# A norm's inverse roots spread through memory, another norm's chain pinned, and the first weights laid side by side, in a hybrid attention layer

## Chip, cores and metric

One core of one Trainium2 chip runs the whole layer. The time is device microseconds of the execution; the median of several runs counts. A profiled execution, taken by the hardware profiler, gives the trace. TensorE is called PE here, VectorE DVE, ScalarE ACT, GpSimd POOL and SyncE SP.

## What is computed

One encoder layer on a sequence of 1024 tokens, width 1024, in float32:

```python
hn = rmsnorm(h, norm_mix)
proj = hn @ w_in                         # 1024 -> 2304, columns for two groups of heads
o_a = window_gqa_sink(rope(qa), rope(ka), va, sink)   # 8 heads, |i-j| <= 128, 2 key heads
o_b = neighbourhood_attention(qb, kb, vb, rpb)        # 8 heads on a 16 x 64 grid
mix = concat([rmsnorm(o_a, norm_a), rmsnorm(o_b, norm_b)])
h = h + mix @ w_out
hn = rmsnorm(h, norm_ffn)
h = h + conv_gated_mlp(hn, w_gate, w_up, conv_w, conv_b, w_down)
return rmsnorm(h, norm_final)

def rmsnorm(x, g):
    return x * rsqrt(mean(x * x, axis=-1) + 1e-6) * g
```

## The kernel before

Everything is held transposed: features lie on the 128 partitions, tokens along the free dimension, so that x is eight tiles of 128x1024 (`KT` = 8). PE multiplies at a reduced float32 precision; the kernel therefore splits each operand into a high part and a low part and makes three products of each pair: high by high, low x by high weights, high x by low weights (`block`, lines 167 to 170). The high part is a copy on ACT, the low part a subtraction on DVE. A tile of 512 tokens (`tsl(h)`, two halves) is the unit of a matmul.

**The order of work.** PE's instructions stand in the order in which the program writes them (`manual_schedule`, line 127). The other engines' instructions are placed by a scheduler, by priority and its own estimate; `tc.high_priority` lifts some, `pin` holds some in program order, and `behind(...)` (line 144) lets an instruction be issued only after a marked one. Each engine executes its own queue strictly in order, SP's queue of DMA issues too, so an instruction that waits holds all behind it.

**The head.** The first three column tiles of `w_in` (`first`, m = 0 to 2) are projected while x arrives. SP issues x and the weights interleaved (lines 88 to 122): the weights of each of the three tiles by themselves, in steps of 1, 1, 2 and 4 row tiles. `split_x` (line 618) makes the two parts of x scaled by the norm's gain, `split_first_w` (line 625) those of the weights, `add_square` (line 631) sums x² over the tiles on ACT and DVE. PE runs nine warming matmuls (`WARM`), then six of the eight row tiles for all three column tiles and both halves (lines 674 to 677). The remaining two (`TAIL`) come tile by tile, and between them stands the first norm: transposes `ss` and a reduce give sums of squares on 128x4 numbers (`inverse_narrow`, line 207), ACT takes the root, DVE the reciprocal, and PE spreads the roots over all partitions by transposes of broadcast columns (`widen`, line 228), `sw` in the trace; ACT copies them to `rstd1`. As the roots are applied after the product (`evacuate`, line 236), the matmuls don't wait for them, but PE's order has `sw` at a fixed place.

**The jobs.** Behind the head stand `jobs`: column tiles 3 to 17 (`Project`) and, as `OutA`, group A's half of the product with `w_out`. `load` fetches and splits the first half of a job's weights, `load_rest` the second; the raw weights have two buffers. The generator `rest` (line 727) hands out the blocks of these jobs one by one, and the attention code pulls them between its own steps, so that PE has work while softmax runs on the other engines. Work of other kinds is hung on fixed blocks of a job by the table `aux` (line 784).

**Between projection and attention.** Tiles of group A are rotated (`rotate`, line 246): DMAs fold the rows on to all partitions (`f<-t`), DVE turns them, DMAs bring them back (`t<-f`). Group B's queries and keys are split and stacked by four DMAs (`split_qk`, line 292). The bias tiles of group B (`bias_tiles`, line 468) are loaded to `rr`, which has one buffer, and built on POOL (`xb`).

**Group A's norm.** After group A's attention, `square_a` sums the squares of four tiles, `narrow_a` adds them up by transposes and takes the inverse roots on 128x8 numbers, `wide_a` spreads them with two sets of PE transposes and two ACT copies to `rstda`, and `normed_a` multiplies each of four tiles, half by half, by gain and root on DVE (lines 757 to 786).

**Tables.** ACT loads a table of functions when it changes from exp to the square root and back.

Of the kernel before, what the change touches and what calls it, by code (L numbers as in the profile page):

```python
# [13 lines left out]
F32 = mybir.dt.float32  # L14
F32R = mybir.dt.float32r
# [21 lines left out]
EVA = (1, 3, 5, 8)  # L37
WARM = 9

# [13 lines left out]

def hybrid_layer(tc, xT, w_in, w_out, w_gate, w_up, w_down, small, sink, rpb, consts, rope, out):
    nc = tc.nc
    with ExitStack() as ctx:
        pool = lambda name, bufs, **kw: ctx.enter_context(tc.tile_pool(name=name, bufs=bufs, **kw))
        cpool = pool("const", 1)
        lpool = pool("long", 1)
        psum = pool("psum", 2, space=PSUM)  # L60
        attention_pools = ctx.enter_context(ExitStack())
        inner = lambda name, bufs: attention_pools.enter_context(tc.tile_pool(name=name, bufs=bufs))
# [28 lines left out]

        def halves(name, dt=F32):
            t = big(name, "mix", dt)[:, :].rearrange("p (k c) -> p k c", c=128)
            return t[:, 0:4], t[:, 4:8]

        raws = [wpool.tile([128, 4, 128], F32, name="raw", tag="raw", bufs=2) for _ in range(2)]
        his, los = ([wpool.tile([128, 4, 128], F32R, name=n, tag=n) for _ in range(3)] for n in ("whi", "wlo"))
        (r3, r3b), r12, h12, l12, (h3, l3) = halves("r3"), halves("r12"), halves("h12", F32R), halves("l12", F32R), halves("w3", F32R)
        head = [list(zip((*raws, r3), his, los)), list(zip((*r12, r3b), (*h12, h3), (*l12, l3)))]

        def load_first_w(m, ks):
            raw, at = head[ks.start // 4][m][0], slice(ks.start % 4, ks.start % 4 + ks.stop - ks.start)
            pin(nc.sync.dma_start(raw[:, at], w_in[m, :, ks, :]))

        steps = [slice(0, 1), slice(1, 2), slice(2, 4), slice(4, 8)]
# [89 lines left out]
        def add_up(v, sq, tag):  # L195

            n = v.shape[-1]
            ps = bank("ss", tag)
            for c in range(n):
                nc.tensor.transpose(ps[:, c * 128:(c + 1) * 128], sq[:, c * 128:(c + 1) * 128], ident)  # L200
            nc.vector.tensor_reduce(v, ps[:, 0:n * 128].rearrange("p (c w) -> p c w", w=128), axis=mybir.AxisListType.X, op=ALU.add)

        def inverse_root(v, dim):
            nc.scalar.activation(v, v, AF.Sqrt, bias=eps, scale=1.0 / dim)
            nc.vector.reciprocal(v, v)

# [84 lines left out]

        def split_qk(t):

            a, b, q = big("ka", "op", F32R), big("kb", "op", F32R), big("q", "op", F32R)
            by = cst[:, K_SCALE:K_SCALE + 1]
            for h in range(2):
                nc.scalar.activation(a[:, tsl(h)], t[:, tsl(h)], AF.Copy, scale=by)
                nc.vector.scalar_tensor_tensor(b[:, tsl(h)], t[:, tsl(h)], by, f32(a[:, tsl(h)]), op0=ALU.mult, op1=ALU.subtract)
            with tc.high_priority(offset=500):
                nc.sync.dma_start(f32(q[0:64, :]), f32(a[0:64, :]))  # L300
                nc.sync.dma_start(f32(q[64:128, :]), f32(b[0:64, :]))
                nc.sync.dma_start(f32(b[0:64, :]), f32(a[64:128, :]))
                nc.sync.dma_start(f32(a[0:64, :]), f32(b[64:128, :]))
            return q, (a, b)
# [64 lines left out]

# [21 lines left out]
        def softmax(st, j, ps, n, bias, nsink=None):  # L391
# [3 lines left out]
            with tc.high_priority(offset=50):  # L395
# [9 lines left out]
                e = n if nsink is None else n + 1  # L405
                nc.scalar.activation(p[:, j, 0:e], p[:, j, 0:e], AF.Exp, bias=nm, scale=-1.0, accum_out=sm[:, j:j + 1])  # L406
                if j == 1:
# [145 lines left out]
        class Project:  # L553
# [3 lines left out]
            def load(self):  # L557
                raw, self.raw = (fetch_w(w_in[self.m, :, k:k + 4, :]) for k in (0, 4))
                self.w = halve_w(raw)
# [64 lines left out]

        def split_first_w(m, ks):
            raw, hi, lo = (t[:, ks.start % 4:ks.start % 4 + ks.stop - ks.start] for t in head[ks.start // 4][m])
            pin(nc.scalar.activation(hi, raw, AF.Copy))  # L627
            pin(nc.vector.tensor_tensor(lo, raw, f32(hi), op=ALU.subtract))
            first[m].w += [(hi[:, j], lo[:, j]) for j in range(ks.stop - ks.start)]

# [12 lines left out]
        for m in range(3):  # L643
            split_first_w(m, steps[0])
        split_x(0, tsl(1))
        for m in range(3):
            split_first_w(m, steps[1])
        for h in range(2):
            split_x(1, tsl(h))
        for m in range(3):  # L650
            split_first_w(m, steps[2])
        acc = add_square(xts[0], None)
        for k in range(2, KT):
            split_x(k)
            if k == 3:
                for m in range(3):
                    split_first_w(m, steps[3])
            acc = add_square(xts[k - 1], acc)
# [193 lines left out]
        for u in range(len(flat)):  # L852
# [14 lines left out]
            for what, e in events:  # L867
# [633 lines left out]
def _layout(inputs):  # L1501
# [9 lines left out]
    rpb[:, ROWS - KH:ROWS + KH - 1] = g["rpb"][0][:, ::-1, ::-1]  # L1511
    consts, rope = _constants()
    arrays = {
        "xT": g["x"][0].T.reshape(KT, 128, S),
        "w_in": blocks(g["w_in"][0][:, _column_order()]),
        "w_out": blocks(g["w_out"][0]),
# [29 lines left out]
```

## Time and profile before

| | us |
|---|---|
| median of 3 runs | 1079.47 (1079.44 to 1079.79) |
| the profiled execution | 1084.39 |
| its span, first to last instruction | 1082.6 |
| PE busy | 1065.0 |
| DVE busy | 867.8 |
| ACT busy | 556.8 |
| POOL busy | 109.9 |
| mean granted clock of TensorE | 0.995 of full speed |

How to read the lines that the prediction shows. In a time line, the first number is the start in us from the start of the span, the second the duration (of all, where several equal ones follow each other: x8), then engine, line of the kernel, operation, what is written <- what is read, shapes, and in brackets the idle time of the engine just before and what ended it. An engine with a q behind it (SPq) is its queue issuing DMAs. Matmuls overlap: the pace is the distance between starts, not the duration. In the list of waits the three numbers are the total in us, how often, and the longest. A row of DMA issues ends with size and median us from issue to landing. A row of windows gives the stretch, its length, the busy time of PE, PEld (weight loads), DVE, ACT and POOL, the granted clock, the busy share of the DMA engines and GB/s.

### The profile page before, as it was taken

The page shows a single profiled execution, that of the slowest core. Times are in us where ns is not written, and L with a number is a line of the kernel's source. Part 1 is how long each engine was busy: PE and PEld are TensorE (multiplying, and loading weights), DVE is VectorE, ACT ScalarE, POOL GpSimd, SP SyncE. Part 2 cuts the span into 40 slices and gives each one's busy share as a digit, 9 for nine tenths or more (in the row PEclk, how much of TensorE's full clock was granted, in tenths as well). Part 3 has the DMA queues.
Part 4 walks back from the last instruction along what each step waited for, and adds up shares of the span by engine and source line. Part 5 has one row for each costly group of instructions (what it writes and reads, how often), then busy time and mean ns, then how long its engine had stood idle before and what let it go on. Part 6 is the DMA issues. An engine that isn't in the chain of part 4 may idle for free.

```text
span 1082.6 us, 14936 instructions
## 1 busy us (share of the span) xinstructions
PE 1065.0 (98%) x5096; PEld 890.0 (82%) x5096; DVE 867.8 (80%) x1599; ACT 556.8 (51%) x1063; POOL 109.9 (10%) x188
## 2 busy tenths in 40 slices
PE   9899999999999999999999999999999999999997
PEld 7688888888888888887788888888888888888886
DVE  6689888667888689899998877877887857897765
ACT  8257777656686545535434334342433645454451
POOL 0323332222233100000000000000000000000001
PEclk9999999999999999999999999999999999999998
DMA  7222122232325146214342222322322789876644
GB/s 276 65 70 70 50 68 69 68 89 68 88 68 163 63 144 244 88 39 165 127 153 101 107 107 97 126 89 108 115 88 98 242 277 309 273 225 231 226 142 156
DMA packets 69084, 144.94 MB, mean 134 GB/s; under 512 B 8208, under 2 KB 19600, under 8 KB 69008
## 3 DMA queue, kind: packets, MB, share of 16 engines
q1 hardware_dynamic: 58784, 118.43, 34.1%
q10 hardware_dynamic: 10224, 25.56, 6.3%
q8 instruction: 40, 0.66, 0.2%
q14 instruction: 36, 0.29, 0.1%
HBM read 103.58 MB, written 28.57 MB: 122 GB/s over the span
## 4 chain that ended last, share of the span: by engine, by line
PE 87%; DVE 8%; DMA 3%; ACT 1%; issue 1%; SPq 0%; POOL 0%; DVEq 0%; ACTq 0%
PE pj L168 7%; PE pj L170 7%; PE pj L169 7%; PE dn L940 6%; PE dn L942 6%; PE dn L941 6%; PE z L942 4%; PE z L940 4%; PE z L941 4%; PE s L380 3%; PE x L940 3%; PE x L941 3%; PE x L942 3%; PE y L942 3%; PE y L940 3%; PE y L941 3%
## 5 line engine op out<-in xcount | busy, mean ns | idle before, releaser
L929 ACT ACTIVATE whi<-ws 128x512 fp32r<-128x512 f32 (+1 forms) x100 | 60.3, 622 | 126.0 <-DVE ws L1047 82.5
L940 PE MATMUL dn<-xd,whi 128*128 128x512 f32 (+1 forms) x330 | 124.0, 376 | 0.0
L942 PE MATMUL dn<-xd,wlo 128*128 128x512 f32 (+1 forms) x330 | 123.7, 375 | 0.0
L941 PE MATMUL dn<-xd,whi 128*128 128x512 f32 (+1 forms) x330 | 123.7, 375 | 0.0
L168 PE MATMUL pj<-xgh,whi 128*128 128x512 f32 x248 | 104.6, 422 | 0.2 <-ACT whi L627 0.2
L942 PE MATMUL z<-hg,wlo 128*128 128x512 f32 x264 | 103.1, 390 | 0.7 <-DVE wlo L930 0.7
L940 PE MATMUL z<-hg,whi 128*128 128x512 f32 x264 | 102.9, 390 | 0.0
L941 PE MATMUL z<-hg,whi 128*128 128x512 f32 x264 | 102.7, 389 | 0.0
L410 POOL TENSOR_SCALAR p<-p,sm 128x384 f32<-128x384 f32 (+1 forms) x128 | 79.8, 637 | 208.6 <-DVE sm L408 167.1
L406 ACT ACTIVATE p<-p,nm 128x385 f32<-128x385 f32 (+3 forms) x128 | 75.2, 587 | 49.8 <-DVE nm L402 48.9
L169 PE MATMUL pj<-xgl,whi 128*128 128x512 f32 x248 | 97.5, 393 | 0.9 <-DVE xgl L623 0.8
L170 PE MATMUL pj<-xgh,wlo 128*128 128x512 f32 x248 | 97.6, 394 | 0.0
L930 DVE TENSOR_TENSOR wlo<-raw,whi 128x512 fp32r<-128x512 f32 (+1 forms) x102 | 66.3, 672 | 26.0 <-ACT whi L929 25.1
L929 ACT ACTIVATE whi<-raw 128x512 fp32r<-128x512 f32 (+1 forms) x102 | 60.5, 612 | 45.5 <-DMA raw<-in_w_down_dram 18.6
L417 DVE TENSOR_TENSOR pl<-pt,ph 128x384 fp32r<-128x384 f32 (+2 forms) x108 | 63.5, 589 | 23.4 <-ACT ph L416 21.7
L930 DVE TENSOR_TENSOR wlo<-ws,whi 128x512 fp32r<-128x512 f32 (+1 forms) x100 | 66.9, 682 | 18.9 <-ACT whi L929 17.7
L1365 POOL TENSOR_TENSOR h<-h,wide 128x256 f32<-128x256 f32 (+1 forms) x6 | 5.4, 919 | 706.9 <-ACT wide L1361 706.9
L416 ACT ACTIVATE ph<-pt 128x384 fp32r<-128x384 f32 (+2 forms) x108 | 55.4, 513 | 31.2 <-PE pt L516 23.8
L942 PEld LDWEIGHTS dn<-xd,wlo 128*128 128x128 f32 x330 | 62.1, 188 | 11.2
L941 PEld LDWEIGHTS dn<-xd,whi 128*128 128x128 f32 x330 | 62.1, 188 | 11.1
L940 PEld LDWEIGHTS dn<-xd,whi 128*128 128x128 f32 x330 | 62.1, 188 | 11.1
L1255 ACT ACTIVATE xd<-xd 128x512 fp32r<-128x512 f32 x77 | 47.5, 627 | 43.5 <-DMA xd<-x 42.9
(231 smaller groups left out, 2677.6 us busy)
## 6 DMA issues: line engine op xcount, KB each, us to landing
xd<-x SPq DMA_DIRECT2D x77, 256.0 KB, 4.7
raw<-in_w_down_dram SPq DMA_DIRECT2D x72, 256.0 KB, 3.8
raw<-in_w_gate_dram SPq DMA_DIRECT2D x22, 512.0 KB, 3.4
raw<-in_w_up_dram SPq DMA_DIRECT2D x22, 512.0 KB, 3.8
x<-c ACTq DMA_DIRECT2D x22, 512.0 KB, 3.7
raw<-in_w_in_dram SPq DMA_DIRECT2D x30, 256.0 KB, 2.9
raw<-in_w_down_dram SPq DMA_DIRECT2D x36, 192.0 KB, 4.2
x<-t ACTq DMA_DIRECT2D x11, 512.0 KB, 2.6
```

Of the source, the lines that this page charges most:

```text
L168: nc.tensor.matmul(ps, w[0], x[0][:, tsl(h)], start=first, stop=False)
L169: nc.tensor.matmul(ps, w[0], x[1][:, tsl(h)], start=False, stop=False)
L170: nc.tensor.matmul(ps, w[1], x[0][:, tsl(h)], start=False, stop=last)
L406: nc.scalar.activation(p[:, j, 0:e], p[:, j, 0:e], AF.Exp, bias=nm, scale=-1.0, accum_out=sm[:, j:j + 1])
L410: nc.gpsimd.tensor_scalar(p[:, i, 0:m], p[:, i, 0:m], sm[:, i:i + 1], 1.0, op0=ALU.mult, op1=ALU.mult)
L416: nc.scalar.activation(ph[:, 0:n], ps[:, 0:n], AF.Copy)
L417: nc.vector.tensor_tensor(pl[:, 0:n], ps[:, 0:n], f32(ph[:, 0:n]), op=ALU.subtract)
L929: nc.scalar.activation(hi, src, AF.Copy)
L930: nc.vector.tensor_tensor(lo, src, f32(hi[:, :, :]), op=ALU.subtract)
L940: nc.tensor.matmul(ps, w[0], x[0], start=first and i == 0, stop=False, skip_group_check=True)
L941: nc.tensor.matmul(ps, w[0], x[1], start=False, stop=False, skip_group_check=True)
L942: nc.tensor.matmul(ps, w[1], x[0], start=False, stop=last and i == len(ws) - 1, skip_group_check=True)
```

## The change

There are four parts. The first weights come as one array `w_first`, laid out so that the three column tiles of a row tile lie side by side (384 columns); five DMAs bring them where twelve did, and 384 columns are split at once, the first high part on DVE. Only the eight gains that the head needs are loaded first. PE starts with three high-by-high products, then the products with low weights, then those with low x. Second, the chain of the first norm (sums, root, reciprocal, the copies of the spread roots) is held in program order, and the second job's first weights may be issued only behind it. Third, group A's roots go to a row in memory and come back as a broadcast row on all partitions, by two DMAs on SP, where transposes and copies spread them before. Fourth, the last split of a query and key (m = 17) has higher priority, and a square root of one number right behind the last exp brings ACT's table early.

```diff
-WARM = 9
+WARM = 8
...
+        FIRST = [slice(0, 1), slice(1, 2), slice(2, 4), slice(4, 6), slice(6, 8)]
...
+        def load_first_w(i):
+            ks = FIRST[i]
+            pin(nc.sync.dma_start(raws[i], w_first[:, ks, :]))
+
+        pin(nc.scalar.dma_start(par[:, 0:KT], small[:, 0:KT]))
         load_x(0, tsl(0))
-        nc.scalar.dma_start(par[:, 0:C_SINK], small)
-        load_x(0, tsl(1), nc.scalar)
-        for m in range(3):
-            load_first_w(m, steps[0])
-        for m in range(3):
-            load_first_w(m, steps[1])
+        load_first_w(0)
+        load_x(0, tsl(1))
+        load_first_w(1)
         load_x(1, tsl(0))
         load_x(1, tsl(1))
-        for m in range(3):
-            load_first_w(m, steps[2])
-        for k in (2, 3):
+        load_first_w(2)
+        for i, k in ((3, 2), (4, 4)):
             load_x(k)
-        for m in range(3):
-            load_first_w(m, steps[3])
-        for k in range(4, KT):
-            load_x(k)
+            load_x(k + 1)
+            load_first_w(i)
+        load_x(6)
+        load_x(7)
+        pin(nc.scalar.dma_start(par[:, KT:C_SINK], small[:, KT:C_SINK]))
...
-        def split_qk(t):
+        def split_qk(t, urgent):
...
             for h in range(2):
-                nc.scalar.activation(a[:, tsl(h)], t[:, tsl(h)], AF.Copy, scale=by)
-                nc.vector.scalar_tensor_tensor(b[:, tsl(h)], t[:, tsl(h)], by, f32(a[:, tsl(h)]), op0=ALU.mult, op1=ALU.subtract)
+                with tc.high_priority(offset=urgent):
+                    nc.scalar.activation(a[:, tsl(h)], t[:, tsl(h)], AF.Copy, scale=by)
+                    nc.vector.scalar_tensor_tensor(b[:, tsl(h)], t[:, tsl(h)], by, f32(a[:, tsl(h)]), op0=ALU.mult, op1=ALU.subtract)
...
-                    qb[h], kb[h] = split_qk(t)
+                    qb[h], kb[h] = split_qk(t, 500 * (m == 17))
...
+        def hi_first_w(k, queue):
+            i, raw = next((i, r) for i, r in enumerate(FIRST) if r.start <= k < r.stop)
+            raw = raws[i][:, k - raw.start]
+            if queue is nc.vector:
+                pin(queue.tensor_copy(his[k], raw))
+            else:
+                pin(queue.activation(his[k], raw, AF.Copy))
+            return raw
+
+        def split_first_w(k, queue=nc.scalar):
+            raw = hi_first_w(k, queue)
+            pin(nc.vector.tensor_tensor(los[k], raw, f32(his[k]), op=ALU.subtract))
+            for p in first:
+                w = slice(128 * p.m, 128 * p.m + 128)
+                p.w.append((his[k][:, w], los[k][:, w]))
...
+        split_first_w(0, nc.vector)
         split_x(0, tsl(0))
...
         for k in range(2, KT):
+            split_first_w(k)
             split_x(k)
...
+        for part in range(3):
+            for p, ps in zip(first, banks):
+                w, x = p.w[0], xg[0]
+                nc.tensor.matmul(ps[0], w[part == 1], x[part == 2][:, tsl(0)], start=part == 0, stop=False)
         for k in range(KT - TAIL):
-            for h in range(2):
+            for h in range(k == 0, 2):
...
                 if p is first[0] and h == 0:
-                    vs1 = [inverse_narrow([acc[:, tsl(i)]], D, "pt") for i in range(2)]
+                    vs1 = [cpool.tile([128, 4], F32, name="v4", tag="v4", bufs=4) for _ in range(2)]
+                    for i in range(2):
+                        pin(add_up(vs1[i], acc[:, tsl(i)], "pt"))
+                    for v in vs1:
+                        root, mark["root"] = inverse_root(v, D)
+                        pin(root)
+                        pin(mark["root"])
                 if p is first[1] and h == 0:
                     for i in range(2):
-                        with tc.high_priority(offset=500):
-                            nc.scalar.activation(rstd1[:, tsl(i)], widen(vs1[i], "pt"), AF.Copy)
+                        mark["spread"] = nc.scalar.activation(rstd1[:, tsl(i)], widen(vs1[i], "pt"), AF.Copy)
+                        pin(mark["spread"])
...
-                    with behind(*["stack"] * (i == 1)):
+                    with behind(*[["spread", "root"], ["stack"]][i] if i < 2 else []):
                         jobs[i + 1].load()
...
+        def spread(dst, v, name):
+
+            row = drams.tile([1, dst.shape[-1]], F32, name=name, tag=name)
+            with tc.high_priority(offset=500):
+                nc.sync.dma_start(row[0, :].rearrange("(c p) -> p c", p=128), v)
+                nc.sync.dma_start(dst, row[0, :].partition_broadcast(128))
+
...
                 if h == 1:
                     inverse_root(norm["v"], 512)
-
-        def wide_a(h):
-            def go():
-                if h == 0:
                     live["op"] += 1
                     norm["a"] = big("rstda", "op")
-                with tc.high_priority(offset=500):
-                    nc.scalar.activation(norm["a"][:, tsl(h)], widen(norm["v"][:, 4 * h:4 * h + 4], "pj"), AF.Copy)
-            return go
+                    spread(norm["a"], norm["v"], "ra")
...
-        aux[11, 8], aux[12, 2], aux[12, 5], aux[12, 11], aux[12, 13] = square_a, narrow_a, narrow_a, wide_a(0), wide_a(1)
+        aux[11, 8], aux[12, 2], aux[12, 5] = square_a, narrow_a, narrow_a
...
+        with tc.high_priority(offset=500), behind("exp"):
+            nc.scalar.activation(warm, eps, AF.Sqrt)
         fill(2)
         pend()
...
+        "w_first": w_in[0:3].transpose(1, 2, 0, 3).reshape(128, KT, 384),
+        "w_in": w_in[3:],
```

More of the change, by code (lines that the diff above doesn't have):

```diff
@@ L51, with hybrid_layer @@
 K_ID, K_MA, K_MB, K_SCALE, K_END = 0, 128, 512, 1152, 1153
-def hybrid_layer(tc, xT, w_in, w_out, w_gate, w_up, w_down, small, sink, rpb, consts, rope, out):
+def hybrid_layer(tc, xT, w_first, w_in, w_out, w_gate, w_up, w_down, small, sink, rpb, consts, rope, out):
     nc = tc.nc
@@ L60, in hybrid_layer @@
         psum = pool("psum", 2, space=PSUM)
+        drams = pool("rows", 1, space=bass.MemoryType.DRAM)
         attention_pools = ctx.enter_context(ExitStack())
@@ L89, in load_x @@
             pin(queue.dma_start(xts[k][:, part], xT[k, :, part]))
[L92 to L105, printed above, removed]
-        load_x(0, tsl(0))
-        nc.scalar.dma_start(par[:, 0:C_SINK], small)
-        load_x(0, tsl(1), nc.scalar)
-        for m in range(3):
-            load_first_w(m, steps[0])
@@ L111, in hybrid_layer @@
-        for m in range(3):
-            load_first_w(m, steps[1])
+        FIRST = [slice(0, 1), slice(1, 2), slice(2, 4), slice(4, 6), slice(6, 8)]
+        flat = lambda t, n: t[:, 0:n * 384].rearrange("p (k c) -> p k c", c=384)
+        raws = [wpool.tile([128, HALF], F32, name="raw", tag="raw", bufs=2) for _ in range(2)]
+        raws = [flat(t[:, :], 1) for t in raws] + [flat(big("r", "op")[:, :], 2) for _ in range(3)]
+        his, los = ([wpool.tile([128, HALF], F32R, name=n, tag=n)[:, 0:384] for _ in range(3)] for n in ("whi", "wlo"))
@@ new lines, in hybrid_layer @@
+        for name, dst, n in (("h", his, 2), ("h", his, 2), ("l", los, 2), ("l", los, 2), ("w", None, 2)):
+            t = flat(big(name, "mix", F32R)[:, :], n)
+            if dst is None:
+                his.append(t[:, 0])
+                los.append(t[:, 1])
+            else:
+                dst += [t[:, 0], t[:, 1]]
+        def load_first_w(i):
+            ks = FIRST[i]
+            pin(nc.sync.dma_start(raws[i], w_first[:, ks, :]))
+        pin(nc.scalar.dma_start(par[:, 0:KT], small[:, 0:KT]))
@@ L200, in add_up @@
                 nc.tensor.transpose(ps[:, c * 128:(c + 1) * 128], sq[:, c * 128:(c + 1) * 128], ident)
-            nc.vector.tensor_reduce(v, ps[:, 0:n * 128].rearrange("p (c w) -> p c w", w=128), axis=mybir.AxisListType.X, op=ALU.add)
+            return nc.vector.tensor_reduce(v, ps[:, 0:n * 128].rearrange("p (c w) -> p c w", w=128), axis=mybir.AxisListType.X, op=ALU.add)
         def inverse_root(v, dim):
-            nc.scalar.activation(v, v, AF.Sqrt, bias=eps, scale=1.0 / dim)
-            nc.vector.reciprocal(v, v)
+            return nc.scalar.activation(v, v, AF.Sqrt, bias=eps, scale=1.0 / dim), nc.vector.reciprocal(v, v)
         def inverse_narrow(sqs, dim, tag, n=4):
@@ L557, in load @@
             def load(self):
-                raw, self.raw = (fetch_w(w_in[self.m, :, k:k + 4, :]) for k in (0, 4))
+                raw, self.raw = (fetch_w(w_in[self.m - 3, :, k:k + 4, :]) for k in (0, 4))
                 self.w = halve_w(raw)
@@ L623, in split_x @@
             pin(nc.vector.scalar_tensor_tensor(lo, src, g, f32(hi), op0=ALU.mult, op1=ALU.subtract))
[L625 to L629, printed above, removed]
+        def hi_first_w(k, queue):
[3 more added lines that the diff above has]
+                pin(queue.tensor_copy(his[k], raw))
+            else:
+                pin(queue.activation(his[k], raw, AF.Copy))
[6 more added lines that the diff above has]
+                p.w.append((his[k][:, w], los[k][:, w]))
         def add_square(t, acc):
```

14 lines of the change are left out of this document (3 added, 11 removed).

## The prediction

> **What bounds the kernel now.** I read the page's busy shares first.
>
> ```profile
> PE 1065.0 (98%) x5096; PEld 890.0 (82%) x5096; DVE 867.8 (80%) x1599; ACT 556.8 (51%) x1063; POOL 109.9 (10%) x188
> ```
>
> TensorE sets the time from end to end. Its matmuls are issued in an order written by hand, so a stall taken out anywhere brings everything behind it forward, as long as the other engines come forward too. So the next view is the list of waits of PE.
>
> ```profile
> PE sw L232 <- DVE v L225: 5.4, 3, 4.6
> PE s L380 <- DMA kb<-ka: 1.1, 1, 1.1
> PE o L528 <- DVE pl L417: 0.9, 1, 0.9
> ```
>
> The change touches all three. The time line around the longest, engine by engine:
>
> ```profile
> 33.21 1.29 DVE L215 TENSOR_REDUCE v<-ss 128x4 f32<-128x512 f32 x2 [0.47 <-PE ss L213]
> 35.97 0.39 PE L170 MATMUL o<-xgh,l 128*128 128x512 f32 x1
> 38.32 0.63 ACT L160 ACTIVATE whi<-raw 128x512 fp32r<-128x512 f32 x1 [9.51 <-DMA raw<-in_w_in_dram]
> 38.97 1.28 ACT L216 ACT_TABLE_LOAD   x1
> 40.26 0.48 ACT L216 ACTIVATE v<-v,eps 128x4 f32<-128x4 f32 x2
> 40.91 1.75 PE L232 MATMUL sw<-cst,v 128*128 128x128 f32 x8 [4.56 <-DVE v L225]
> 42.32 0.78 PE L168 MATMUL o<-xgh,h 128*128 128x512 f32 x1
> 44.97 0.39 PE L168 MATMUL s<-xgh,w 128*128 128x512 f32 x1
> 47.69 1.03 PE L325 MATMUL vt<-cst,t 128*128 128x128 f32 x8
> ```
>
> The sums of squares stood ready at 34.50 (33.21+1.29). ACT, idle for 9.51 us, waited for the weights of the second job behind the head, which stand ahead of the square root in its program. PE came to the spreading transposes at about 36.20 and got the roots at 40.91. Then it ran slow: six 512-column matmuls took 2.65 us from 42.32 to 44.97, twelve more 2.72 from there to 47.69, 0.227 each.
>
> ```profile
> 41.00:46.00 5.00, 4.96 (x19) 4.07 (x20) 3.11 (x6) 1.20 (x2) 0.00 (x0) 0.66 0.34 106
> ```
>
> The granted clock in that stretch is 0.66 (the third column from the end); it is a cost of the stall and goes with it.
>
> **The change, part by part.** All sums are made on the profiled execution (1084.39 us, span 1082.6); the median of the runs is 1079.47, 4.92 less, and I carry the difference over.
>
> *First norm pinned.* In the changed order of ACT the square root and both spreading copies stand ahead of the late weights. The table load before the root isn't late instead: one in mid-attention began before its operand was there.
>
> ```profile
> 279.15 0.67 DVE L201 TENSOR_REDUCE v<-ss 128x4 f32<-128x512 f32 x1
> 279.43 1.28 ACT L204 ACT_TABLE_LOAD   x1
> 281.44 0.19 DVE L205 RECIPROCAL v<-v 128x8 f32<-128x8 f32 x1
> ```
>
> Reduce 279.82, load from 279.43. So after reduce (34.50 in the old clock) come a root of 0.24 and a reciprocal of 0.19, about 35.0, before PE's 36.20: the wait of 4.71 goes, and 2.65 − 6×0.227 = 1.29 of slow matmuls, and of the transposes 0.6 (40.91 to 42.32 is 1.41, against 0.8 for two sets at the pace quoted for group A below). Together 6.6. What is late next is the sum of squares on DVE, priced as a rival.
>
> *First weights side by side.* Rows:
>
> ```profile
> 4.87 0.50 PE L168 MATMUL pj<-xgh,whi 128*128 128x512 f32 x1 [0.21 <-ACT whi L627]
> 5.80 0.40 PE L170 MATMUL pj<-xgh,wlo 128*128 128x512 f32 x1
> 12.45 1.15 ACT L622 ACTIVATE xgh<-xt,par 128x1024 fp32r<-128x1024 f32 x1 [0.97 <-DMA xt<-in_xT_dram]
> 13.64 1.29 DVE L623 SCALAR_TENSOR_TENSOR xgl<-xt,par,xgh 128x1024 fp32r<-128x1024 f32 x1 [2.40 <-ACT xgh L622]
> 13.66 0.50 PE L168 MATMUL pj<-xgh,whi 128*128 128x512 f32 x1
> 14.98 0.50 PE L169 MATMUL pj<-xgl,whi 128*128 128x512 f32 x1 [0.82 <-DVE xgl L623]
> 0.00:20.00 20.00, 17.89 (x77) 14.46 (x78) 11.50 (x20) 15.06 (x25) 0.44 (x6) 1.00 0.88 306
> ```
>
> Twelve weight DMAs become five, at the same bytes, and their conversions go from 12 pairs to 8. The third x tile, which landed at 12.45 and held PE from 13.66 to 14.98, is issued eighth instead of thirteenth on SP; PE reaches it around 12.8 (4.67 and 36 matmuls of 0.227) and it should land near 9.5 (some 2.3 MB stand before its end, at the 306 GB/s of this stretch, from about 2). So 1.32−0.23 = 1.1 goes. The start: the third matmul begins 0.93 after the first, at pace 0.45, so 0.48 goes because the three products of high halves now stand first; and the weights' high half is made on DVE, free then, beside ACT's x. Its copy of 384 columns isn't in the trace: between nothing and 0.51 (a subtraction of 512, wlo below, costs 0.68, so three quarters of it); I take 0.35 and an earlier start of 0.2; were the 192 KB in one piece to land later than the first 64 KB did, it could be 0.3 the other way. Eight warming matmuls for nine cost nothing while they end (about 4.3) just before the first real one. Sum 1.8; with the first part 8.4, so vt at 39.3 instead of 47.69.
>
> *What follows the head.* Each SP instruction behind a moved wait counts here. The new SP order puts the fold DMAs of the rotary step (f) behind the third bias load and a weight load, and both bias loads wait for POOL.
>
> ```profile
> 27.33 4.78 POOL L480 TENSOR_TENSOR xb<-cst,rr 128x384 f32<-128x384 f32 x1 [26.36 <-DMA rr<-in_rpb_dram]
> 33.34 0.55 SPq L472 DMA_DIRECT2D rr<-in_rpb_dram  x1
> 37.67 0.98 POOL L480 TENSOR_TENSOR xb<-cst,rr 128x384 f32<-128x384 f32 x1 [3.75 <-DMA rr<-in_rpb_dram]
> 39.34 0.55 SPq L472 DMA_DIRECT2D rr<-in_rpb_dram  x1
> 44.06 2.41 SPq L254 DMA_DIRECT2D f<-t  x2
> 49.09 0.47 DVE L256 TENSOR_TENSOR f<-f,turns 64x128 f32<-64x128 f32 x2
> 60.31 0.68 DVE L161 TENSOR_TENSOR wlo<-raw,whi 128x512 fp32r<-128x512 f32 x1
> 62.20 0.39 PE L168 MATMUL pj<-xgh,whi 128*128 128x512 f32 x1
> h1d<-h ACTq DMA_DIRECT2D x16, 256.0 KB, 2.1
> ```
>
> POOL's first bias tile took 4.78 beside an unbroken DVE, the second 0.98 beside an idle one. If it ends when DVE's sums end, which I put 2.8 earlier than before (DVE's idle 2.40 ahead of the third tile goes, and some 0.4 at the start), the second bias load goes out at 30.5, the third 6.0 later (33.34 to 39.34), the fold about 1.2 after that at 37.7, landing at 39.8 (2.1, the shortest time of a store to landing) to 42 (behind the 4.33 that a bias load took, 33.34 to 37.67). The rotation keeps pace with PE if it starts by 49.09−8.4 = 40.7, and may be 1.6 later: its last user, wlo, ends at 60.99, and PE wants it two matmuls behind 62.20. Cost 0 to 1; I take 0.3. On ACT the late weights now stand ahead of the other half of the folds and of the value copies. They landed 4.98 after the second bias load went out (33.34 to 38.32), so now about 35.5, and nothing is held.
>
> The Trainium skill, page "SBUF — State Buffer", section "Who interferes with whom", says that a DVE instruction with two SBUF inputs shuts out a GpSimd instruction that reads SBUF, for the whole instruction. 4.78 against 0.98 agrees. Without that rule POOL would be done by about 24 and the 0.3 would be 0; with it, this sum stands.
>
> *Group A's roots.* Two sets of transposes leave PE, two copies leave ACT:
>
> ```profile
> 285.41 0.61 PE L232 MATMUL sw<-cst,v 128*128 128x128 f32 x4
> 285.78 0.47 PE L168 MATMUL pj<-xgh,whi 128*128 128x512 f32 x1
> 286.96 1.73 DVE L781 SCALAR_TENSOR_TENSOR mixa<-mixa,par,rstda 128x512 f32<-128x512 f32 x2
> x<-c ACTq DMA_DIRECT2D x22, 512.0 KB, 3.7
> h<-h1d SPq DMA_DIRECT2D x16, 256.0 KB, 5.3
> ```
>
> One set costs PE 0.37 from its start to the next, 0.4 with what it slows behind it: 0.8 for both. In DVE's new order one product with the root stands where two stood, and two of the eight go some 30 instructions later, so the 0.9 wait of o for pl, which stands seven microseconds behind these products, should halve: 0.5. New is a wait: DVE stops at the first product until two transfers, one after the other, have landed; behind it stand the softmax of the next scores and the next probabilities, for which PE waits. No transfer of 1024 separate words is in the trace. Bounds: 2.1 twice (the shorter store, taken for the load too) and 3.7+5.3 (the longer store, the longest load); I take 5.4, near the first, as little is moved. Root at 281.63, landed 287.0, wanted about 288.2: free up to 6.6, while 9.0 would hold DVE 2.4. SP, which waits between the two, holds back only weights that are used a job later.
>
> *Last key split urgent.* The chain of waits ahead of the 1.1 us of PE is two transfers:
>
> ```profile
> 337.71 3.18 DMA q<-kb
> 340.91 4.67 DMA kb<-ka
> ```
>
> In DVE's new order the second half's kb, which lets the first go, stands right behind the first half's, ahead of two additions and a score step; the transfers follow it. But on SP one x load more now stands ahead of each pair of them. Between 0 and 1.2; I take 0.7, nearer the whole wait.
>
> *Square root's table early.* 5.4−4.6 = 0.8 of PE's wait for roots is left for two others, after the last attention. The table load there (1.28, as at 38.97) moves to a gap of ACT: 0.4.
>
> Sum: 8.4−0.3+0.8+0.5+0.7+0.4 = 10.5. 1084.39−10.5 = 1073.9 profiled, 1069.0 as the median.
>
> **The rivals.**
> - *SP held longer by POOL*: if POOL ends no earlier than before (33.3), the fold lands 2.8 later, PE stands 2 us at the second job's weights: 1071. For it: 4.78. Against: it followed DVE, which comes forward.
> - *DVE's sums are late*: pinned or not, the roots need them. If DVE comes no earlier than before, the roots are there at 35.0 and 35.2, while PE, 1.8 ahead of its old clock, wants them at 34.4; with its own wait at the sums it stands about 1.2: 1070.2.
> - *Transfers late*: at 9.0 the group A gain turns into a loss: the 0.5 not gained, and 1 to 2.4 for the hold: 1070.5 to 1072.
> - *Slower*: the same wait, with 1024 words moved one by one. A hold of 2.4 cost PE about 1 before; to eat 10.5 and 2.2 more the round trip must take over 20 us. Then 1082 and up. Only its small pieces speak for it; no transfer in these rows takes half of that.
> - *All hidden*: the 0.3, and what is left of the waits for pl (0.4), kb (0.5) and the start, about 1.7 in all: 1067.3.
>
> The Trainium skill, "DMA: Bandwidth & Descriptors", "Rules for kernel authors", warns that a non-contiguous last dimension becomes one descriptor per element, which is what the first transfer does. By it the transfers come later than I take them, up to the two rivals above; no run so far shows its price.
>
> **How the numbers follow.** Forecast 0.46; SP 0.14; sums 0.14; transfers 0.12; all hidden 0.10; slower 0.04. A measurement of this kernel tells 0.2% (2.2 us) from no change. Faster 0.95; same 0.02 (round trips of 16 to 20 us); slower 0.03. The range takes in "all hidden" and the transfers at 9.0: 1066.8 to 1073.3.
>
> **What would show it.** In the changed profile: no wait of PE for the first roots, granted clock 1.00 from 30 to 45, vt near 39.3; x tile three before PE; the first product with rstda starting at once after the probabilities; no wait of s for kb. A PE wait at the second job's weights is the first rival, one at ss or sw the second, an idle DVE before L781's successor the third. Wrong would be any of these above 2 us.

## The result, and the profile after

The changed kernel is slower: 1085.94 us, the median of 10 runs (1084.88 to 1088.69), against 1080.93 for the kernel before (10 runs, 1078.3 to 1087.03); ratio 1.0045, 95% interval 1.003 to 1.006. The forecast was 1069.0 and faster. The profiled executions stand closer, 1085.42 after and 1084.39 before, because the one of before was a long one; that turns out to matter.

First the list of waits of TensorE in the changed kernel (columns: in total, times, longest):

```profile
PE o L529 <- ACT ph L418: 7.6, 1, 7.6
PE o L530 <- DVE pl L419: 1.8, 3, 0.9
PE sw L233 <- DVE v L226: 0.6, 1, 0.6
PE ss L202 <- DVE sq L647: 0.2, 1, 0.2
```

The 4.6 us at the first roots and the 1.1 at kb are gone, as forecast (the 0.6 at sw is the last norm's, at 1077; it stands in every profile here). In their place stands one stop of 7.6 us, in the middle of attention. The time line around it, all engines:

```profile
273.46 0.19 DVE L206 RECIPROCAL v<-v 128x8 f32<-128x8 f32 x1
273.68 0.39 SPq L780 DMA_DIRECT2D ra<-v  x1
274.17 0.54 SPq L304 DMA_DIRECT2D kb<-ka  x1
...
279.27 0.56 DVE L419 TENSOR_TENSOR pl<-pt,ph 128x384 fp32r<-128x384 f32 x1 [0.23 <-ACT ph L418]
...
283.81 0.40 PE L172 MATMUL pj<-xgh,wlo 128*128 128x512 f32 x1
284.41 0.34 SPq L781 DMA_DIRECT2D rstda<-ra  x1
...
288.29 0.75 DVE L798 SCALAR_TENSOR_TENSOR mixa<-mixa,par,rstda 128x512 f32<-128x512 f32 x1 [8.45 <-DMA rstda<-ra]
288.95 0.55 DVE L404 CUSTOM_DVE_ANT_0 p<-s,xb 128x384 f32<-128x384 f32 x1
...
289.55 0.61 ACT L408 ACTIVATE p<-p,nm 128x384 f32<-128x384 f32 x1 [8.35 <-DVE nm L404]
...
291.30 0.74 ACT L418 ACTIVATE ph<-pt 128x384 fp32r<-128x384 f32 x2
291.82 0.69 PE L529 MATMUL o<-ph,v 128*128 128x384 f32 x1 [7.62 <-ACT ph L418]
293.28 0.69 PE L530 MATMUL o<-pl,v 128*128 128x384 f32 x1 [0.77 <-DVE pl L419]
```

Read it from the top. The roots stand at 273.65. The store ra goes out at once. SP may issue the load only when the store has landed: 284.41. VectorE has come to the first product with rstda at 279.83 and stands in front of it for 8.45 us. Behind it in VectorE's program stands the softmax of the next scores (288.95), for which ScalarE waits 8.35, and for ScalarE TensorE 7.62. The wait list names ScalarE; the cause is three steps back, a transfer.

The transfers by themselves (issue, KB, us from the start of the issue to landing), and the packets that started from 273.6 to 276.6, then from 276.6 to 284.3:

```profile
rstda<-ra SPq DMA_DIRECT2D x1, 512.0 KB, 3.9
ra<-v SPq DMA_DIRECT2D x1, 4.0 KB, 10.7
```

```profile
DMA packets 1241, 0.49 MB, mean 165 GB/s; under 512 B 1058, under 2 KB 1179, under 8 KB 1241
DMA packets 17, 0.02 MB, mean 2 GB/s; under 512 B 14, under 2 KB 14, under 8 KB 16
```

The store of 4 KB took 10.7, the load of 512 KB 3.9. Its 1024 words had started by 276.6, all but a few at most (1058 packets under 512 B, 14 more later), and in the 7.7 us until it landed next to nothing new did (17 packets). So it is not handing out the words that took long, but what lies between that and the report of the landing. The engines were not wholly idle meanwhile: six packets of 4 KB that had started by 276.7, of the transfer of k behind the store, stayed open for 2.0 to 5.5 us, where most of its packets took 0.3. The Trainium skill, page "DMA: Bandwidth & Descriptors", section "Anatomy of one DMA — SWDGE (gpsimd) path", says that a transfer's semaphore can only fire when the last byte is confirmed in the memory it goes to, and that most of a transfer's fixed time of some 2 us is this. That section is about transfers that GpSimd issues, these two go out from SyncE; a landing 7.7 us behind the words agrees with it in kind, not in size.

The stop also costs clock. Third column from the end, granted clock, in the stop and behind it:

```profile
283.80:291.80 8.00, 0.40 (x2) 0.00 (x0) 3.45 (x8) 2.25 (x7) 0.00 (x0) 0.75 0.31 98
291.80:298.30 6.50, 5.70 (x19) 4.65 (x19) 4.83 (x11) 0.87 (x3) 1.43 (x2) 0.52 0.13 43
```

To sum it I compare the distance from each matmul's start to the next with the usual distance of such a pair in the same trace, and add up the excess ("lag"). From 280 to 300 the lag is 11.7 us; before, it was 2.1. In the first 60 us it is 3.15 against 10.6. So the head gained 7.5 between these two profiles, and the stretch around group A's norm lost 9.6.

### The profile page after: what moved, and what is told of

Read it like the earlier page. It is cut to its first block, busy times and chain, and to the rows that moved or that the text cites. A ratio compares the mean times of both kernels' runs of the same rounds, so it can differ in the third digit from the quotient of the medians.

```text
span 1083.6 us, 14896 instructions
## 1 busy us (share of the span) xinstructions
PE 1064.4 (98%) x5086; PEld 889.7 (82%) x5086; DVE 867.6 (80%) x1596; ACT 554.7 (51%) x1057; POOL 108.6 (10%) x188
## 4 chain that ended last, share of the span: by engine, by line
PE 85%; DVE 9%; ACT 2%; DMA 2%; issue 1%; POOL 0%; DVEq 0%; SPq 0%; ACTq 0%
PE pj L170 7%; PE pj L172 7%; PE pj L171 7%; PE dn L959 6%; PE dn L961 6%; PE dn L960 6%; PE z L961 5%; PE z L960 5%; PE z L959 5%; PE s L382 3%; PE x L960 3%; PE x L959 3%; PE x L961 3%; PE y L961 3%; PE y L960 3%; PE y L959 3%
## 5 line engine op out<-in xcount | busy, mean ns | idle before, releaser
L960 PEld LDWEIGHTS dn<-xd,whi 128*128 128x128 f32 x330 | 62.1, 188 | 11.1
L959 PEld LDWEIGHTS dn<-xd,whi 128*128 128x128 f32 x330 | 62.1, 188 | 11.1
```

Source lines behind the costliest of these rows:

```text
L959: nc.tensor.matmul(ps, w[0], x[0], start=first and i == 0, stop=False, skip_group_check=True)
L960: nc.tensor.matmul(ps, w[0], x[1], start=False, stop=False, skip_group_check=True)
```

## The experiments

All are variants of the changed kernel, if not said otherwise. My theory: the store of separate words alone loses the time. Rivals: a stop that would be there anyway, the queue, the strided load, a fixed time of any small store.

**The old spreading in the changed kernel.**

```diff
-                    spread(norm["a"], norm["v"], "ra")
...
+                    nc.scalar.activation(norm["a"][:, tsl(h)], widen(norm["v"][:, 4 * h:4 * h + 4], "pj"), AF.Copy)
```

> The changed kernel with one part undone: group A's inverse roots are spread by transposes on TensorE and copies on ScalarE again; the head and all else stay changed. Theory (the two transfers alone lose what the head gained): the stop of TensorE of 7.6 us at o goes, and what runs slow behind it; of the 11.7 us by which the matmuls from 280 to 300 lag their own usual pace some 2.1 remain, as in the kernel before. From 1085.9 that takes off 9.6 and gives back 0.9 for eight transposes: 1077, 4 below before's 1080.9. Rival (the stop would be there without the transfers, since the earlier head makes softmax late): 1083 or more, with a wait of o for ph of several us at the same place.

1076.62 (5 runs; before beside it 1079.97), ratio 0.9966 (0.9954 to 0.9979). No stop near 284; the lag from 280 to 300 is 2.16. The stop comes with the transfers.

**The transfers alone in the kernel before.**

```diff
-        aux[11, 8], aux[12, 2], aux[12, 5], aux[12, 11], aux[12, 13] = square_a, narrow_a, narrow_a, wide_a(0), wide_a(1)
+        aux[11, 8], aux[12, 2], aux[12, 5] = square_a, narrow_a, narrow_a
+                    spread(norm["a"], norm["v"], "ra")
```

> The kernel before with one part of the change alone: group A's roots by two transfers through memory. Theory: the same stop of TensorE of 7 to 8 us behind VectorE's first product with rstda, and the slow matmuls after it; before plus 9.6 less 0.9 for eight transposes, about 1089 to 1090. Rival (the stop comes of the shifted head and not of the transfers): within 2 us of before, 1079 to 1083.

1089.72 (4 runs; before beside it 1079.97), ratio 1.0088 (1.007 to 1.0107), with the same stop. Waits of TensorE:

```profile
PE o L528 <- ACT ph L417: 7.5, 1, 7.5
PE s L381 <- DMA kb<-ka: 3.0, 1, 3.0
PE sw L233 <- DVE v L226: 1.7, 3, 0.8
```

The last line is a surprise: this kernel has the head of before, and yet the first roots (its longest wait) cost 0.8, not 4.6. Below, that becomes an experiment.

**The same 4 KB in pieces of 32 bytes.**

```diff
-                nc.sync.dma_start(row[0, :].rearrange("(c p) -> p c", p=128), v)
+                nc.sync.dma_start(row[0, :].rearrange("(p c) -> p c", p=128), v)
```

and the products read the row with a stride of eight words.

> The changed kernel, the row in memory in another order: each partition's eight roots lie side by side, so the store is 128 pieces of 32 bytes instead of 1024 words; the products read the row with a stride of eight words. The order of all instructions stays as it is. Theory (time goes by the number of separate words written, 10.3 us for 1024, 64 for each of 16 engines): an eighth of the pieces, the store from issue to landing 2 to 3.5 us instead of 10.3, the load 3.5 as it was, VectorE's wait at the first product 8.45 - 7 to 8 = about 1, TensorE nearly without a stop: 1076 to 1078. Rival (the store waits behind the bias load and the transfers of k on the same queue, whatever its pieces): the store still takes about 10, 1084 to 1087. Second rival (the strided reading makes each of eight products longer, and they stand before the probabilities): products of 1.5 us instead of 0.75, up to 6 us on VectorE, 1078 to 1082.

1078.50 (11 runs), ratio 0.9984 (0.9975 to 0.9993). The store takes 2.2, the load 3.6:

```profile
rstda<-ra SPq DMA_DIRECT2D x1, 512.0 KB, 3.6
ra<-v SPq DMA_DIRECT2D x1, 4.0 KB, 2.2
```

The roots stood at 274.26, the row at 280.23: a round trip of 6.0, and VectorE didn't wait. On the same queue, behind the same bias load, the store is five times as fast; the queue is out. But the second rival had a part: each strided product took 1.25 instead of 0.75, and the lag from 280 to 300 is 4.1.

**Eight rows of 512 bytes.** One transpose of the roots (128x8 to 8x128) on TensorE and one copy ahead of the store:

```diff
+                nc.tensor.transpose(ps[0:8, 0:128], v, ident)
+                nc.vector.tensor_copy(turned, ps[0:8, 0:128])
-                nc.sync.dma_start(row[0, :].rearrange("(c p) -> p c", p=128), v)
+                nc.sync.dma_start(row[0, :].rearrange("(c p) -> c p", p=128), turned)
```

> The changed kernel, the roots turned first: one transpose on TensorE and a copy on VectorE make 8 rows of 512 bytes, stored as 8 pieces, then the same broadcast load. The order of the first products changes by one score step. Theory (number of words written): the store lands within 2 to 3 us; it starts about 1.5 us later, so the product waits 0 to 2 us: 1076 to 1079. Rival (the queue, whatever the pieces): the store still takes about 10, 1084 to 1089.

1075.31 (5 runs, 1073.98 to 1076.9), ratio 0.9956 (0.9942 to 0.9969): faster than both kernels. Its time line:

```profile
274.21 0.19 DVE L206 RECIPROCAL v<-v 128x8 f32<-128x8 f32 x1
...
274.66 0.27 PE L782 MATMUL sw<-cst,v 128*8 128x128 f32 x1
274.99 0.27 DVE L783 COPY turned<-sw 8x128 f32<-8x128 f32 x1
275.28 0.31 SPq L784 DMA_DIRECT2D ra<-turned  x1
277.56 0.34 SPq L785 DMA_DIRECT2D rstda<-ra  x1
...
281.23 1.41 DVE L804 SCALAR_TENSOR_TENSOR mixa<-mixa,par,rstda 128x512 f32<-128x512 f32 x2
```

The store landed by 277.56, 2.3 after its issue; the row was there at 281.21, and the product started with no wait shown, but also with nothing to spare. One score step of VectorE now stands ahead of it. The lag from 280 to 300 is 0.95.

**Half the words, and the words apart.** Three kernels ask what made the store slow: 512 words instead of 1024; 1024 words 64 bytes apart; 1024 words 16 bytes apart.

```diff
-                nc.sync.dma_start(row[0, :].rearrange("(c p) -> p c", p=128), v)
+                nc.sync.dma_start(row[0, 0:512].rearrange("(c p) -> p c", p=128), v[:, 0:4])
...
+                nc.sync.dma_start(row[0, :].rearrange("(c p s) -> p c s", p=128, s=16)[:, :, 0:1], v)
...
+                nc.sync.dma_start(row[0, :].rearrange("(c p s) -> p c s", p=128, s=4)[:, :, 0:1], v)
```

> The changed kernel, with half of the store: the roots of the first 512 columns alone are stored, as 512 separate words, and the row is loaded twice, for both halves (the second half of group A is scaled by the wrong roots). Theory (time by the number of words, 10.3 us for 1024): the store takes about 5 to 5.5 us from issue to landing, VectorE waits 3 to 4 at the first product. Rival (a fixed time of about 10 for any store of separate words, or a wait for something else on the queue): 9 to 10.5.

> The changed kernel, each of the 1024 words on 64 bytes of its own in a row of 64 KB, filled early from x; the load then takes the first 4 KB of that row (so group A is scaled by other numbers than the roots). It tells apart why separate words are slow. Theory A (each word costs its time, wherever it goes): the store takes 10 us as in the changed kernel, VectorE waits 8 to 9. Theory B (sixteen words of a row's 64 bytes come from sixteen partitions, and writes into the same 64 bytes wait for each other): 2 to 4 us, VectorE waits 0 to 2.

> The changed kernel, each word on 16 bytes of its own: four words in 64 bytes instead of sixteen (the load takes the first 4 KB of a row filled early from x, so group A is scaled by other numbers). 1024 adjacent words took 10.3 us, 512 adjacent 9.3, 1024 words 64 bytes apart 2.6. Theory B (the words that share 64 bytes wait for each other, about 0.5 us each): four in a row, the store takes 3 to 5 us. Rival (any sharing costs the same, or what counts is the span of memory and not the sharing): 8 to 10, or 2.6 as at 64 bytes.

From the issue to landing, in this order:

```profile
ra<-v SPq DMA_DIRECT2D x1, 2.0 KB, 9.7
```

```profile
ra<-v SPq DMA_DIRECT2D x1, 4.0 KB, 2.9
```

```profile
ra<-v SPq DMA_DIRECT2D x1, 4.0 KB, 3.4
```

The theory by number of words falls: half of them take 9.7 instead of 10.7, and all of them, 64 bytes apart, 2.9. In these runs, what costs is that words next to each other in memory are written singly: 4 KB side by side in pieces of 32 bytes took 2.2. "Each of those that share 64 bytes waits about 0.5" fits sixteen (10.7) but is too slow for four: 2.9 plus three more of 0.5 would be 4.4, and they took 3.4 (counted from the end of the issue, as the expectation counted, 2.97, 2.56 and 10.28). Between four and sixteen neighbours lies a jump, and why is open; whether it matters that neighbouring words come from different partitions isn't separated either. The Trainium skill, "DMA: Bandwidth & Descriptors", "Rules for kernel authors", warns of one descriptor per element. The 1058 small packets above agree; these three stores all break that rule, and one in three is dear. By time (one run each) 1087.14, 1077.09 and 1076.66.

**The slow store, but nobody waiting.** The products stand behind the next job's first copy out of PSUM.

```diff
+                with behind("late"):
                     nc.vector.scalar_tensor_tensor(
                         mix[i][:, tsl(h)], mix[i][:, tsl(h)], col(C_NA + i), norm["a"][:, tsl(h)], op0=ALU.mult, op1=ALU.mult)
```

> The changed kernel with its store of 1024 adjacent words left as it is, but VectorE's products with the roots stand only behind the next job's first copy out of PSUM, some 12 us later in its program. Theory (the store costs nothing by itself; the loss is the instruction that stands waiting at the head of VectorE's queue): the store still takes 10 us, VectorE doesn't wait for rstda, TensorE has no stop near 284: 1075 to 1077. Rival (the slow store also holds SP and the transfers behind it, and these stop TensorE): a new wait for k or for weights of 2 us or more, 1079 to 1085.

1084.07 (12 runs), ratio 1.003 (1.0016 to 1.0044). Half a miss: the store still took 10.7 from the end of its issue (11.1 from its start), VectorE didn't wait for it, there is no stop near 284, and the lag from 280 to 300 is 1.5. But 30 us later there are two others:

```profile
PE s L382 <- DMA kb<-ka: 3.2, 1, 3.2
PE s L382 <- DMA ka<-kb: 2.8, 1, 2.8
```

```profile
306.03 0.75 DVE L800 SCALAR_TENSOR_TENSOR mixa<-mixa,par,rstda 128x512 f32<-128x512 f32 x1
...
308.41 0.74 DVE L300 SCALAR_TENSOR_TENSOR kb<-t,cst,ka 128x512 fp32r<-128x512 f32 x1
...
311.92 0.74 DVE L300 SCALAR_TENSOR_TENSOR kb<-t,cst,ka 128x512 fp32r<-128x512 f32 x1
...
312.69 0.47 SPq L303 DMA_DIRECT2D q<-kb  x1
313.25 0.55 SPq L305 DMA_DIRECT2D ka<-kb  x1
...
317.17 0.36 PE L382 MATMUL s<-ka,q 128*128 128x256 f32 x1 [2.84 <-DMA ka<-kb]
```

The eight products now run up to the last key split on VectorE. Its second half starts at 311.92 and ends at 312.66, with other work between the halves; in the kernel with the rows both halves were done at 307.29 (305.88 + 1.41). Its transfers follow late. So the rival's number and its wait for k came, but by another way: the store did hold SP (the load went out at 285.03, the next weights at 285.42, against 279.94 in the kernel with the rows), and no wait of TensorE follows from that; the wait for k follows from the products that now stand ahead of the split. No run moves the products and has a fast store, so this last step rests on the time line alone.

**Is the long wait in the head usual?** The kernel before, unchanged, for another profile; and the pinned chain alone in it.

```diff
-                    vs1 = [inverse_narrow([acc[:, tsl(i)]], D, "pt") for i in range(2)]
+                        root, mark["root"] = inverse_root(v, D)
+                        pin(root)
...
+                        pin(mark["spread"])
```

> The kernel before, unchanged, for another profile of it. In its first profile (1084.4, 4.9 above the median that stood beside it) TensorE waited 4.6 us at sw for the first roots; with the same head the kernel with the transfers alone showed 0.8. Theory (that long wait is one execution's: GpSimd's first bias tile took 4.78 us there and 2.05 in the other, and the weights behind it landed late): here a wait at sw of 0 to 2 us, and a time of 1078 to 1082. Rival (the wait is this kernel's own, and the transfers or the bias tile's place make the difference): 4 to 5 us again, at 1083 to 1086.

> The kernel before with the chain of the first norm pinned, alone: square root and spreading copies ahead of the late weights. The forecast priced this at 6.6 us. Theory (the price was read from one execution with a long wait; the usual wait is near 0.8 to 1): 1 to 3 us faster than before, 1077 to 1079. Rival (the price holds): 6 to 7 faster, 1073 to 1074.

The kernel before showed this in its second profile (1080.27; GpSimd's first bias tile, ScalarE, TensorE at the first roots):

```profile
26.46 2.25 POOL L480 TENSOR_TENSOR xb<-cst,rr 128x384 f32<-128x384 f32 x1 [25.49 <-DMA rr<-in_rpb_dram]
...
34.99 0.63 ACT L160 ACTIVATE whi<-raw 128x512 fp32r<-128x512 f32 x1 [5.52 <-DMA raw<-in_w_in_dram]
...
37.59 1.29 PE L232 MATMUL sw<-cst,v 128*128 128x128 f32 x8 [0.51 <-DVE v L225]
```

0.5 where the first profile had 4.6. The bias tile took 2.25, not 4.78; SP, which waits for GpSimd there, sent the late weights earlier; ScalarE converted them at 34.99, not 38.32. With the kernel with the transfers alone (0.8; bias tile 2.05) and the one below (0.4; 2.30) that makes three profiles without the long wait against one. It need not be rare: of the 63 unchanged executions of the kernel before that stand beside all these runs, six took over 1084 us, and what made those long no trace shows.

The pinned chain alone is worth accordingly: 1078.51 (11 runs) against 1079.69, ratio 0.9992 (0.9983 to 1.0001). That is about 1 us where the forecast had 6.6, and the interval still holds no change at all. None of before's 15 runs beside it was a long one (highest 1080.86).

**The first weights alone** in the kernel before:

```diff
+            pin(nc.sync.dma_start(raws[i], w_first[:, ks, :]))
...
+        split_first_w(0, nc.vector)
```

> The kernel before with the first weights side by side alone (with the order of the first products that goes with it). The forecast priced it at 1.8: no stop at the third x tile and an earlier start. With the pinned chain alone at 0.9 +- 1.1 below before, and the changed kernel with the old spreading at 3.4 below, theory: 1.5 to 2.5 faster than before, no wait of pj for xgl at the third tile. Rival (a gain in the head is taken by the wait for the first roots, since TensorE reaches them earlier): 0 to 0.5 faster, with the wait at sw longer by 1.5 to 2.

1078.04 (12 runs; before 1080.22), ratio 0.9971 (0.9959 to 0.9984): the theory. The wait for xgl is gone, and the first roots cost 0.4, so they weren't made late by it.

**The two small parts left out** of the kernel with the rows:

```diff
-                    qb[h], kb[h] = split_qk(t, 500 * (m == 17))
+                    qb[h], kb[h] = split_qk(t)
...
-            nc.scalar.activation(warm, eps, AF.Sqrt)
```

> The best kernel so far (the changed one, with the roots turned and stored as 8 rows of 512 bytes: 1075.3) without the two small parts: the last key split is not made urgent and the square root's table is not loaded early. The forecast priced them at 0.7 and 0.4. Theory (both are mostly taken by waits of o for pl that remain): 1075 to 1076, a wait for kb of about 1 us back, and one of sw by 0.4 to 0.7. Rival (the prices hold): 1076.3 or more, by 1.1 slower than with them.

1075.00 (6 runs), ratio 0.9949 (0.9931 to 0.9967), against 1075.31 with them in another series: no difference that shows. The wait for kb is back (first fence, without the parts), and with them stands another in its place (second fence):

```profile
PE s L382 <- DMA kb<-ka: 1.4, 1, 1.4
```

```profile
PE o L530 <- DVE pl L419: 1.0, 2, 0.9
```

## Why the prediction was wrong

*Group A's roots* is the step that turned the sign. Of its terms the 0.8 for eight transposes and 0.5 for the wait for pl hold: with a fast store in place of the old spreading the time fell from 1076.62 to 1075.31, 1.3 as forecast (the intervals overlap; that the 1.02 us of lag at o before pl is gone shows in the trace). "Free up to 6.6" holds too: VectorE came to the product 6.2 after the roots. And the round trip of 5.4 was near what two transfers with a fast store need, 6.0 and, with the turning, 6.8 (274.40 to 281.21). What failed is the store: bounded between 2.1 and 3.7 by rows that were all of long pieces, and 10.7 with single neighbouring words. The prediction named exactly that ("1024 words moved one by one") and then gave it 0.04, because no transfer in the rows took so long. But no transfer in the rows was of that kind either.

The rival *Slower* had its point of decision too high: over 20 us of round trip to lose, and 14.6 did it (273.65 to 288.26). Its "a hold of 2.4 cost PE about 1" doesn't give the 20: by it the 12.7 to be eaten (10.5 and 2.2) ask for 30 us of hold and 37 of round trip. At one to one they make 6.6 + 12.7 = 19.3. Both other terms were off: the gains to be eaten were not 10.5 but about 4.7 (below), and the hold cost more than itself. Once VectorE's 6.2 us of slack were used up, 8.45 of hold became 7.8 of stop, 1.3 at the next wait and slow matmuls at a clock of 0.52, together 11.7 of lag against 0.95 in the kernel with the rows. An idle VectorE before the first product was the prediction's own sign of *Transfers late*; that rival had the right place, and priced it at 1 to 2.4.

*First norm pinned* is the second step that failed: it had the mechanism right and the size wrong, 6.6 forecast and about 1 measured. Profile against profile it came as written: no wait at the first roots, and a granted clock (third column from the end) of 1.00 over the stretch in which it had fallen to 0.66,

```profile
30.00:45.00 15.00, 14.83 (x79) 12.25 (x78) 11.73 (x28) 4.45 (x9) 2.50 (x9) 1.00 0.40 110
```

and the value transposes at 39.99, forecast 39.3. But the wait that went was that of one long execution. With it goes "I carry the difference over": the 4.92 between that execution and the median was this very wait with the slow matmuls behind it, so its removal could not be subtracted from the median a second time. Over the first 60 us the lag of the first profile of before is 10.6, of the second 5.8: 4.9 apart. Later medians of before, 1079.69 to 1080.22, say the same.

*First weights side by side*: 1.8 forecast, 2.2 by medians. Right. *What follows the head*: the cost of near nothing came, and the fold transfers went out at 37.59, forecast 37.7, but the time is luck. The forecast had them 1.2 behind a third bias load at 36.5; that load went out at 34.52, GpSimd's first tile taking 2.73, and what they waited for was VectorE's tile t, done at 37.56:

```profile
34.52 0.54 SPq L474 DMA_DIRECT2D rr<-in_rpb_dram  x1
36.27 1.29 DVE L239 TENSOR_TENSOR t<-pj,rstd 128x512 f32<-128x512 f32 x2 [2.41 <-ACT rstd L703]
37.59 1.79 SPq L255 DMA_DIRECT2D f<-t  x2
```

No wait stands at the second job's weights. The rivals *SP held longer* and *DVE's sums are late* didn't come about; TensorE waited 0.2 at the sums.

*Last key split urgent* (0.7) and *square root's table early* (0.4): nothing measurable. The wait for kb goes, and a wait for pl of 0.9 comes at the same stage. Of the 0.8 that was "left for two others" only 0.24 stood right behind the attention (at 383.69), less than the 0.4 forecast, and it goes; the other 0.64 is the last norm's, at the kernel's end.

So with the measured terms: 1079.97 - 1.2 - 2.2 - 1.3 = 1075.3, and the kernel with the rows has 1075.31. The changed one stands 10.6 above that; its lag from 280 to 300 is 11.7 against 0.95, 10.8 more. Against medians of before, 10.5 faster was forecast and 5.0 slower came: of these 15.5 the store makes 10.6 and the first norm's price 5.4, 0.5 too much together, which lies within the spread between the series.

## What to carry to other kernels

A transfer of single words is bounded by no row of long pieces: where the trace has none of its kind, its price is open upwards and the chance of a loss isn't small. Turn the data first, so that each partition writes one long run. A profiled execution that lies well above the median of the runs has its excess somewhere in it: look for it before you price the longest stall, and never take the stall and keep the offset. And a wait on an in-order engine costs nothing until its slack is gone, then all of it.

## What was not expected of the hardware

Store of 4 KB in single words: 10.7 us with words side by side, 3.4 at 16 bytes' distance, 2.9 at 64, 2.2 in pieces of 32 bytes; half as many side by side, 9.7. While it hung, the transfer of k issued behind it (274.17) hung too and landed at 284.50, and the bias load issued ahead of it (272.17) at 281.75. In the kernel with pieces of 32 bytes, with the same order of issues, they landed at 277.73 and 276.35. So one slow store holds up what runs beside it.

GpSimd's bias tile took 4.78, 2.25 and 2.05 us in three profiles with the same VectorE instructions beside it, and 1.76 to 3.06 in the other profiles. In the profile with 4.78 the VectorE instructions beside it kept their usual lengths (1.27, 1.21, 0.68, 1.21), until a small one at 31.18 took 0.96 instead of 0.16; in the one with 2.25, one at 27.77 took 2.03 instead of 1.28. So it looks as if GpSimd gets on where a VectorE instruction is held up, and why at this one and not at another is open. The Trainium skill, page "SBUF — State Buffer", section "Who interferes with whom", says that the two shut each other out and that the order of issue decides who waits. The trace agrees that one holds up the other; the order of issue it doesn't show.
